# Hybrid encoder on one core: order of the mirrored Fourier rows, and smaller edits of the Fourier weights

## The chip, the cores and the metric

The kernel runs on one core of one Trainium2 chip. A core has five engines with a queue each: PE (TensorE, matmuls), DVE (VectorE), ACT (ScalarE), POOL (GpSimd) and SP (SyncE, which here only issues DMAs). The metric is the device time of one execution in microseconds (us); a run's result is compared by the median of several executions. The profile shows one execution. Its span runs from the first instruction to the last.

## The reference

Two layers over a sequence of 512 tokens of width 1024, in float32. Each layer is a half-step SwiGLU block, a mixer, and another half-step SwiGLU block; a final RMSNorm follows. The mixer is what the change touches:

```python
def fourier_mix(u):
    ug = u.astype(jnp.float32).reshape(B, T, F_GROUPS, F_GROUP_DIM)
    f = jnp.fft.fft2(ug, axes=(1, 3), norm="ortho").real
    return f.reshape(B, T, F_WIDTH).astype(u.dtype)

def mixer(h, w_in, gate_bias, rpb, w_na_out, w_f_out, w_o):
    z = h @ w_in                       # q, k, v, uf, ga, gf
    y_na = neighbourhood_attention(q, k, v, rpb) @ w_na_out
    y_f = fourier_mix(uf) @ w_f_out
    g_na = sigmoid(ga + gate_bias[0])
    g_f = sigmoid(gf + gate_bias[1])
    return (g_na * y_na + g_f * y_f) @ w_o
```

The neighbourhood attention has 8 heads of 64; the Fourier part has 4 groups of 128 channels; `ga` and `gf` are 1024 wide each.

## The kernel before

**Matmuls in three parts.** Every float32 operand of a large matmul is split into a high part (rounded to float32r, an ACT copy) and a low part (the rest, a DVE subtraction). A product is high times high, high times low and low times high. For weights, `Item.prep` makes the two parts `whi` (ACT, L207 or L202) and `wlo` (DVE, L210 or L203), each 128 x 1024, in three rotating buffers.

**Strassen products.** The large products are done by seven half-size products, numbered 1 to 7 (`strassen`, `product`). The weights come as granules of 128 x 1024 floats (512 KB), two per product. A granule serves 12 matmuls. Some products need sums of granules a, b, c, d: for product 7 the sum c + a, for product 5 the sum d + c, for product 6 that sum plus a, for product 3 also plus b. SP loads a granule from `wst` into a raw buffer (L155). `plus` then has POOL issue a DMA that adds a second granule to the buffer as it lands (L165); `then` (L212) does the same later, once the first use is over; other sums are made by DVE (L179).

**The stream of weights.** All items stand in one list. `Stream.prep` prepares items in order, and before each one fetches items up to `depth` (8) ahead. `next` hands out an item and prepares two items further. An item carries a stage number; it is not fetched before `enter` has raised the stage. In the mixer the raw buffers come from the shared pool of 23 buffers of 4 KB per partition (`slot`), which also holds activations, probabilities, Fourier results and the gate bias. `swap_pools(0)` closes the mixer's own pool and puts 9 raw buffers in its place; these serve the gates and the next block.

**Attention and Fourier part** (from L1695). PE, DVE and ACT run here in the order in which the program is written (`manual_schedule`). Eight blocks of attention (`Probs` 0 to 7: scores, `maxes`, `exps`, `inverse`, `scaled`, `transposed`, `kept`, and `att_pv` for two blocks at a time) are interleaved with the Fourier part:

- The transform along the tokens and channels uses symmetry. `four_high` and `four_ends` leave the even-odd halves `yf`, the end rows `e_` and the Nyquist column `nyq`.
- `part_f(0, ...)` multiplies the even half with the even weights (granules t1 + t2, added by POOL), and `part_f(1, ...)` the odd half with the odd weights (t1 - t2, loaded anew and subtracted by DVE). In `part_f(0, ...)` two more matmuls (L1653, L1654) bring in the end rows with the high and the low part of the ends' weights `fx`, which `ends_split` makes.
- `last_f` makes the Nyquist row in three partial products of 32 rows each; `f_last` copies them out of PSUM and has POOL add the three rows into row 3 of `fs[i, 0]` by DMAs of 2 KB.
- `f_both` makes, for each token, the sum into `gs` and the difference into `fs`. The rows of `gs` belong to mirrored tokens. `f_turn(i)` sends them to their places in `fs[i, .]` by eight DMAs on SP: four of 60 rows and four of 3 or 4 rows, 2 KB per row.

`i` is the half of the output columns (0 or 1).

**Gates.** `fill` multiplies attention's output with its first weights. Then `gate_block(0)` and `gate_block(1)` make both gates for a half of the columns each; block 0 takes its products in the order `FIRST`, block 1 in the order `ORDER`. After products 1 and 6 a `snap` copies the PSUM pair out by ACT (L619), and a later product adds to the same PSUM pair. `with_f` (product 7 and product 4) multiplies the gate into `fs` (DVE, L1539), so it needs the mirrored rows. `minus` and what follows it prepares the activations of products 5, 6, 7 and 4 (t1, t2, t3, t4). In this stretch DVE and ACT are ordered by the program only as far as its `manual_schedule` blocks reach; SP's order is not written out anywhere, the framework's scheduler sets it. Each engine runs its queue in order. After block 0, its two results are turned to channels by a DMA transpose on SP (`zt<-zs`, L376) and joined by ACT (L389).

In the program of before, `f_turn(0)`, `f_turn(1)` come at the end of the attention part, ahead of `fill`; the two bias loads `gb` (L1892) follow `fill`. They stand ahead of the loads of the gate's c granules.

Of the kernel before, what the change touches and what calls it, by code (L numbers as in the profile page):

```python
# [98 lines left out]
def encoder_kernel(  # L99
# [67 lines left out]
    class Item:  # L167
        def __init__(self, raw, add=None, neg=False, stage=0, parts=1, pieces=1, then=None, op=ALU.add):
            self.raw, self.add, self.neg, self.stage, self.parts, self.op = raw, add, neg, stage, parts, op
            self.pieces, self.then = pieces, then  # L170
# [6 lines left out]
        def summed(self):  # L177
            if self.add:
                V.tensor_tensor(self.raw.t, self.raw.t, self.add.t, self.op)  # L179
                self.add = None  # L180
# [14 lines left out]
        def prep(self, nxt):  # L195
# [8 lines left out]
            else:  # L204
                for c in range(0, n, n // self.parts):
                    cs = slice(c, c + n // self.parts)
                    S.activation(hi[:, cs], t[:, cs], AF.Copy)  # L207
                    if nxt:
                        nxt.summed()
                    self.last = V.tensor_tensor(lo[:, cs], t[:, cs], hi[:, cs].bitcast(F32), ALU.subtract)  # L210
# [6 lines left out]
    def stage_items():  # L217
# [5 lines left out]
        def strassen(s, name, idx, sizes, order, dma=False, behind=None):  # L223
# [4 lines left out]
            for q, q2 in (("a", None), ("b", None), ("c", "a"), ("d", "c")):  # L228
                r[q] = [Raw(key(q, g), n, q2 and key(q2, g)) for g, n in enumerate(sizes)]
# [5 lines left out]
            for m, g in at:  # L235
# [13 lines left out]
                else:  # L249
                    add(c)  # L250
# [19 lines left out]
        for l in range(L):  # L270
# [17 lines left out]
            for i in range(2):  # L288
                strassen(s, lambda q: "g" + q, i, two, ORDER if i else FIRST, True)
# [834 lines left out]
    def stage_mixer(l, norm, nxt):  # L1124
# [5 lines left out]
        ch = mp.tile([P, 164], F32, tag="ch", name=nm("ch"), bufs=1)  # L1130
# [221 lines left out]
        def four_high(ps, z):  # L1352
# [7 lines left out]
            def low_of():  # L1360
# [6 lines left out]
                V.tensor_copy(nyq[:, z, 0:1], ps[:, 256:257])  # L1367
# [4 lines left out]
        def four_ends(ps):  # L1372
# [7 lines left out]
            def low_of():  # L1380
                V.scalar_tensor_tensor(e_, g.bitcast(F32), ch[:, 162:163], t, ALU.mult, ALU.add)
                V.tensor_tensor(nyq[:, 2, 0:1], ps[:, 256:257], ch[:, 160:161], ALU.mult)
# [252 lines left out]
        def ends_split():  # L1635
            t = ends[0]
            h, l_ = hilo("fxh"), hilo("fxl")
            for i in range(2):
                S.activation(h[i], t[:, i], AF.Copy)
            for i in range(2):  # L1640
                V.tensor_tensor(l_[i], t[:, i], h[i].bitcast(F32), ALU.subtract)
            ends.extend([h, l_])

        def part_f(m, t, w, i=None):
# [7 lines left out]
            if m == 0:  # L1652
                PE.matmul(ps, e_[:, c], ends[1][i], start=False, stop=False)  # L1653
                PE.matmul(ps, e_[:, c], ends[2][i], start=False, stop=True)  # L1654
# [28 lines left out]
        def f_last(i, ps):  # L1683

            t = tmp(s="fl")
            V.tensor_copy(t[0:96], ps[0:96])
            to = fs[i, 0][3:4, 1, :]
            for z in range(3):
                row = t[32 * z : 32 * z + 1]
                if z == 0:  # L1690
                    G.dma_start(out=to, in_=row)
                else:
                    G.dma_start(out=to, in_=row, accum_op=ALU.add)

        with tc.manual_schedule(engines={mybir.EngineType.DVE, mybir.EngineType.Activation}):  # L1695
            with tc.manual_schedule(engines={mybir.EngineType.PE}):
# [71 lines left out]
                p[4].maxes(1)  # L1768
                q3 = q3()
# [24 lines left out]
                pf = [part_f(0, t, f_w[0], 0) for t in range(2)]  # L1794
                att_split(po[0])
# [7 lines left out]
                f_copy(0, 1, pf[1])  # L1803
                pt_[4] = kept(ts)
# [4 lines left out]
                att_split(po[1])  # L1809
                p[6].maxes(0)  # L1810
# [20 lines left out]
                for i in range(2):  # L1831
                    f_last(i, pl[i])
# [26 lines left out]
                f_turn(0)  # L1859
                f_turn(1)  # L1860
# [27 lines left out]
        bias = []  # L1888
        for which in range(2):
            b_ = slot(F32, "gb", (D,))  # L1890
            src = bass.AP(tensor=gbias.tensor, offset=gbias.offset + (2 * l + which) * D, ap=[[0, P], [1, D]])
            nc.sync.dma_start(out=b_, in_=src)  # L1892
            bias.append(b_)

# [9 lines left out]
        def fourth():  # L1904
            with behind_weights():
# [142 lines left out]
def _weights(g):  # L2048
    wst = np.zeros((len(GRAN), P, 1024), np.float32)
    for l in range(L):  # L2050
# [38 lines left out]
        for i in range(2):  # L2089
            four("g", i, ga, i * T, gf, i * T)  # L2090
            wf = g["f_w_out"][l][:, i * T : (i + 1) * T].reshape(4, P, T)
            for z in range(2):
                for e in range(2):
# [3 lines left out]
                    wst[GRAN_AT[s, "f", 4], 32 * (2 * z + e) : 32 * (2 * z + e) + 2, i * T : (i + 1) * T] = m[64]  # L2097
# [61 lines left out]
def _constants():  # L2159
# [12 lines left out]
    chan = np.zeros((P, 164), np.float32)  # L2172
    chan[:, 0:64], chan[:, 64:128] = np.cos(ca) / 256.0, np.sin(ca) / 256.0
    chan[:, 128:130] = (1.0 - 2.0 * (np.arange(P) % 2))[:, None] / 256.0
    chan[0::32, 160] = chan[0::32, 162] = 1.0
    chan[1::32, 161], chan[1::32, 162] = 1.0, -1.0
# [35 lines left out]
```

## Time and profile before

| | us |
|---|---|
| median of 3 runs | 1859.37 (1856.95 to 1862.17) |
| the profiled execution | 1860.03 |
| its span | 1858.3 |
| DVE busy | 1604.3 |
| ACT busy | 1306.1 |
| POOL busy | 187.7 |

The profile page gives the busy time of each engine and, in 40 slices of 46.5 us, its busy share in tenths. A timeline row gives start, duration, engine, line, operation, the tiles (output <- inputs, without buffer numbers), shapes and a count; in brackets stands the idle time of the engine just before and what ended it. In the chain of waits, each row is a piece of the chain that ended last: its start, its length and what it was. SPq rows are SP's issuing of DMAs; the transfer itself runs later. In a row of a stretch come the engines' busy times, then PE's granted clock (1.00 is full), the busy share of the DMA engines and what they moved in GB/s. Matmul durations overlap: at full clock one follows another every 0.227 us, though each is listed with 0.39.

### The profile page before, as it was taken

Reading aid. Unit: us, or ns where it says so; the run is one execution under the profiler, and the core shown is the slowest. Engines: PE = TensorE matmul, PEld = TensorE weight load, DVE = VectorE, ACT = ScalarE, POOL = GpSimd, SP = SyncE. Lnnn points to the kernel's source line nnn. Section 1 sums busy time; section 2 is a strip of 40 time slices with the busy share of each in tenths; the row PEclk is TensorE's granted clock in tenths of the full one; section 3 lists DMA queues with packets and bytes.
Section 4 is the critical chain, followed back from the end, with each engine's and each line's share of the span. In section 5 each row is a group of like instructions: output and inputs, shape, how many; then the busy total and the mean of one; then the engine's idle time right before and its main releaser. Section 6 shows DMA issues by size and latency. Waiting matters only on the chain.

```text
span 1858.3 us, 24537 instructions
## 1 busy us (share of the span) xinstructions
PE 1829.5 (98%) x8778; PEld 1514.2 (81%) x8778; DVE 1604.3 (86%) x1938; ACT 1306.1 (70%) x1775; POOL 187.7 (10%) x231
## 2 busy tenths in 40 slices
PE   9999999999899999999999999999998899999998
PEld 7888888887778888888888888888877788888886
DVE  7878899777889987889998888997788799888899
ACT  6777875677576777787667778666675677677865
POOL 0001010110111010001010100101011101110010
PEclk9999999999999999999999999999999999999999
DMA  9898799862987788869878986978539877888695
GB/s 304 223 242 213 187 280 285 205 199 85 283 217 183 167 229 241 215 198 279 249 190 214 226 224 202 282 251 226 160 124 273 214 181 177 219 232 215 200 286 157
DMA packets 206770, 405.87 MB, mean 218 GB/s; under 512 B 109116, under 2 KB 109276, under 8 KB 206648
## 3 DMA queue, kind: packets, MB, share of 16 engines
q1 hardware_dynamic: 176536, 302.61, 50.5%
q0 software_dynamic: 29680, 101.14, 29.9%
q8 instruction: 69, 1.13, 0.3%
q10 hardware_dynamic: 432, 0.55, 0.1%
q14 instruction: 53, 0.43, 0.1%
HBM read 372.76 MB, written 2.11 MB: 202 GB/s over the span
## 4 chain that ended last, share of the span: by engine, by line
PE 90%; DMA 4%; DVE 3%; ACT 2%; issue 1%; SPq 0%; ACTq 0%; DVEq 0%
PE A L534 10%; PE A L537 10%; PE A L535 10%; PE o L537 7%; PE o L534 7%; PE o L535 7%; PE B L534 5%; PE B L535 5%; PE B L537 5%; DMA raw<-in_wst_dram 2%; PE C L534 2%; PE C L535 2%; PE C L537 2%; PE ps L339 2%; PE ps L340 2%; PE ps L341 2%
## 5 line engine op out<-in xcount | busy, mean ns | idle before, releaser
L210 DVE TENSOR_TENSOR wlo<-raw,whi 128x1024 fp32r<-128x1024 f32 (+1 forms) x534 | 632.6, 1196 | 181.0 <-ACT whi L207 177.5
L207 ACT ACTIVATE whi<-raw 128x1024 fp32r<-128x1024 f32 (+1 forms) x534 | 546.7, 1033 | 292.4 <-PE A L535 60.4
L165 POOL DMA_DIRECT2D raw<-in_wst_dram x170 | 148.9, 895 | 1218.4 <-DMA raw<-in_wst_dram 636.3
L179 DVE TENSOR_TENSOR raw<-raw,raw 128x1024 f32<-128x1024 f32 (+1 forms) x152 | 181.6, 1197 | 2.0
L535 PE MATMUL A<-whi,xl 128*128 128x512 f32 x400 | 155.7, 389 | 0.0
L534 PE MATMUL A<-whi,xh 128*128 128x512 f32 x400 | 155.7, 389 | 0.0
L202 ACT ACTIVATE whi<-raw 128x1024 fp32r<-128x1024 f32 (+1 forms) x83 | 85.7, 1037 | 46.9 <-PE A L535 11.4
L389 ACT ACTIVATE at<-zt 128x1024 uint16<-128x1024 uint16 (+2 forms) x96 | 110.3, 1166 | 11.3 <-DMA zt<-zs 11.3
L537 PE MATMUL A<-wlo,xh 128*128 128x512 f32 x400 | 115.0, 389 | 0.0
L203 DVE SCALAR_TENSOR_TENSOR wlo<-raw,whi 128x1024 fp32r<-128x1024 f32 (+1 forms) x83 | 98.8, 1198 | 12.3 <-ACT whi L202 12.3
L537 PEld LDWEIGHTS A<-wlo,xh 128*128 128x128 f32 x400 | 75.1, 188 | 15.6
L534 PEld LDWEIGHTS A<-whi,xh 128*128 128x128 f32 x400 | 75.1, 188 | 15.4
L535 PEld LDWEIGHTS A<-whi,xl 128*128 128x128 f32 x400 | 75.1, 188 | 15.4
L534 PE MATMUL B<-whi,xh 128*128 128x512 f32 x208 | 81.2, 390 | 0.0
L535 PE MATMUL B<-whi,xl 128*128 128x512 f32 x208 | 81.0, 389 | 0.0
L535 PE MATMUL C<-whi,xl 128*128 128x512 f32 x208 | 81.0, 389 | 0.0
L534 PE MATMUL C<-whi,xh 128*128 128x512 f32 x208 | 80.9, 389 | 0.0
L370 ACT ACTIVATE zs<-th 128x1024 uint16<-128x1024 uint16 x80 | 79.4, 1040 | 0.4 <-DVE th L794 0.4
L787 ACT ACTIVATE th<-sn,rh 128x512 f32<-128x512 f32 x80 | 54.8, 715 | 31.2 <-DVE sn L624 30.3
L619 ACT ACTIVATE sn<-A 128x512 f32<-128x512 f32 x104 | 58.4, 584 | 22.9 <-PE A L537 22.9
L537 PE MATMUL C<-wlo,xh 128*128 128x512 f32 x208 | 59.8, 389 | 0.0
L537 PE MATMUL B<-wlo,xh 128*128 128x512 f32 x208 | 59.8, 389 | 0.0
(446 smaller groups left out, 4641.4 us busy)
## 6 DMA issues: line engine op xcount, KB each, us to landing
raw<-in_wst_dram SPq DMA_DIRECT2D x472, 512.0 KB, 6.0
raw<-in_wst_dram POOLq DMA_DIRECT2D x180, 512.0 KB, 8.1
bm<-in_bias_dram SPq DMA_DIRECT2D x16, 512.0 KB, 5.9
raw<-in_wst_dram SPq DMA_DIRECT2D x30, 256.0 KB, 5.9
vs<-v SPq DMA_DIRECT2D x24, 128.0 KB, 5.6
x<-in_xin_dram SPq DMA_DIRECT2D x4, 512.0 KB, 10.2
raw<-in_wst_dram POOLq DMA_DIRECT2D x8, 256.0 KB, 7.4
dft<-in_dft_dram POOLq DMA_DIRECT2D x8, 256.0 KB, 6.7
```

Source lines behind the costliest of these rows:

```text
L165: G.dma_start(out=self.t, in_=wst[GRAN_AT[self.plus]][:, 0 : self.n], accum_op=ALU.add)
L179: V.tensor_tensor(self.raw.t, self.raw.t, self.add.t, self.op)
L202: S.activation(hi, t, AF.Copy, scale=-1.0)
L203: self.last = V.scalar_tensor_tensor(lo, t, -1.0, hi.bitcast(F32), ALU.mult, ALU.subtract)
L207: S.activation(hi[:, cs], t[:, cs], AF.Copy)
L210: self.last = V.tensor_tensor(lo[:, cs], t[:, cs], hi[:, cs].bitcast(F32), ALU.subtract)
L370: S.activation(s[:, h], words[:, h], AF.Copy)
L389: S.activation(to[:, w], t[:, w], AF.Copy)
L534: PE.matmul(ps, lh, rh, start=start, stop=False, skip_group_check=again)
L535: PE.matmul(ps, ll, rh, start=False, stop=False, skip_group_check=again)
L537: PE.matmul(ps, lh, rl, start=False, stop=stop, skip_group_check=again)
L619: S.activation(t[:, b, :], ps[b], AF.Copy)
```

## The change

It has five parts.

1. **Mirrored rows and order.** `f_turn(0)` moves from the end of the attention part to the gates, behind the first three weights of `fill` and a new `ws.fetch(ws.prepped + 9)`. `f_turn(1)` moves into `fourth`, which runs after product 6 of gate block 0. The two bias loads move ahead of both.
2. **Odd Fourier weights in place.** t1 isn't loaded a second time. The raw buffer that holds t1 + t2 gets -2 x t2 added by one DVE instruction (`scalar_tensor_tensor`), after the even product and `last_f` have read it. `last_f(0)` comes earlier for this, right behind `part_f(0, ., 0)`; the second odd sum is called by hand after `p[7].maxes`.
3. **Ends' weights in one product.** The three products high x high, low x high and high x low of the end rows are laid in three rows of one matmul: the row of `fx` now stands three times, `ch` has one more column, and `ends_split` makes a tile with high, high and low parts in rows 0, 1 and 2 of each group of 32. One matmul in `part_f(0, ...)` goes, so four per layer.
4. **Nyquist row by DVE.** The Nyquist column stands in column 3 of `nyq`, so that the row comes out in row 3 of each 32. `f_last` copies 96 x 512 as before; two DVE additions over 32 x 512 write rows 0 to 31 of `fs[i, 0]`, and the later `f_turn` overwrites those that are not the Nyquist row.
5. **Order in the attention part.** The first two `minus` steps move from behind `p[7].scaled` to behind `p[4].maxes`; `ws.enter` comes before `p[7].maxes`; the second odd weight is prepared ahead of `p[7].scaled`. A new argument `on_chip` of `strassen` is passed as False and changes nothing.

```diff
@@ class Item
+                if self.twice:
+                    V.scalar_tensor_tensor(self.raw.t, self.add.t, -2.0, self.raw.t, ALU.mult, ALU.add)
+                else:
+                    V.tensor_tensor(self.raw.t, self.raw.t, self.add.t, ALU.add)
...
-                    if nxt:
+                    if nxt and not nxt.twice:
                         nxt.summed()
@@ stage_items
-            for t1, t2 in halves:
-                add(Raw(t1, plus=t2))
-            for t1, t2 in halves:
-                add(Raw(t1), Raw(t2), op=ALU.subtract)
+            even = [Raw(t1, plus=t2) for t1, t2 in halves]
+            for raw in even:
+                add(raw)
+            for raw, (_, t2) in zip(even, halves):
+                add(raw, Raw(t2), twice=True)
@@ four_high, four_ends
-                V.tensor_copy(nyq[:, z, 0:1], ps[:, 256:257])
+                V.tensor_copy(nyq[:, z, 3:4], ps[:, 256:257])
@@ ends_split
-            t = ends[0]
-            h, l_ = hilo("fxh"), hilo("fxl")
-            for i in range(2):
-                S.activation(h[i], t[:, i], AF.Copy)
-            for i in range(2):
-                V.tensor_tensor(l_[i], t[:, i], h[i].bitcast(F32), ALU.subtract)
-            ends.extend([h, l_])
+            t, h, z = ends[0], slot(F32R, "fxh", (2, T)), slot(F32, "fxz", (2, T))
+            S.activation(h, t, AF.Copy)
+            S.activation(z, t, AF.Copy, scale=ch[:, 163:164])
+
+            def low_of():
+                V.scalar_tensor_tensor(h, h.bitcast(F32), ch[:, 164:165], z, ALU.mult, ALU.add)
+
+            ends.append(h)
+            return low_of
@@ part_f
-                PE.matmul(ps, e_[:, c], ends[1][i], start=False, stop=False)
-                PE.matmul(ps, e_[:, c], ends[2][i], start=False, stop=True)
+                PE.matmul(ps, e_[:, c], ends[1][:, i], start=False, stop=True)
@@ f_last
-            t = tmp(s="fl")
+            t, to = tmp(s="fl"), fs[i, 0][0:32, 1, :]
             V.tensor_copy(t[0:96], ps[0:96])
-            to = fs[i, 0][3:4, 1, :]
-            for z in range(3):
-                row = t[32 * z : 32 * z + 1]
-                if z == 0:
-                    G.dma_start(out=to, in_=row)
-                else:
-                    G.dma_start(out=to, in_=row, accum_op=ALU.add)
+
+            def added():
+                V.tensor_tensor(to, t[0:32], t[32:64], ALU.add)
+                V.tensor_tensor(to, to, t[64:96], ALU.add)
+
+            return added
@@ attention part, in its order
                 p[4].maxes(1)
+                first = minus(B[0, 0], B[0, 1], "t1")
+                next(first)
+                next(first)
...
-                ends_split()
+                low = ends_split()
                 p[4].inverse(0)
                 p[4].inverse(1)
+                low()
...
                 pf = [part_f(0, t, f_w[0], 0) for t in range(2)]
+                pl = [last_f(0, raws[0])]
...
                 f_copy(0, 1, pf[1])
+                fl = f_last(0, pl[0])
...
                 att_split(po[1])
+                fl()
...
-                pl = [last_f(i, raws[i]) for i in range(2)]
+                pl.append(last_f(1, raws[1]))
+                ws.enter(ws.stage + 1)
                 p[7].maxes(0)
                 p[7].maxes(1)
+                ws.items[ws.prepped].summed()
...
-                for i in range(2):
-                    f_last(i, pl[i])
+                fl = f_last(1, pl[1])
...
                 p[7].inverse(1)
+                ws.prep(ws.pos + 2)
+                fl()
                 p[7].scaled(0)
                 p[7].scaled(1)
-                first = minus(B[0, 0], B[0, 1], "t1")
-                next(first)
-                next(first)
                 pt_[6] = kept(ts)
                 att_split(po[2])
-                ws.enter(ws.stage + 1)
...
                 f_both(1, 1, pf[1])
-                f_turn(0)
-                f_turn(1)
@@ gates
+        bias = []
+        for which in range(2):
+            b_ = slot(F32, "gb", (D,))
+            src = bass.AP(tensor=gbias.tensor, offset=gbias.offset + (2 * l + which) * D, ap=[[0, P], [1, D]])
+            nc.sync.dma_start(out=b_, in_=src)
+            bias.append(b_)
+
             w = [ws.next(0), ws.next(0)]
             ws.prep(ws.pos + 1)
+            ws.fetch(ws.prepped + 9)
+            f_turn(0)
             h1 = high(t12, "t1")
...
         def fourth():
+            f_turn(1)
             with behind_weights():
```

(The bias loads stood behind this block before.)

More of the change, by code (lines that the diff above doesn't have):

```diff
@@ L167, in encoder_kernel, with __init__ @@
     class Item:
[L168 to L169 removed]
+        def __init__(self, raw, add=None, neg=False, stage=0, parts=1, pieces=1, then=None, twice=False):
+            self.raw, self.add, self.neg, self.stage, self.parts, self.twice = raw, add, neg, stage, parts, twice
             self.pieces, self.then = pieces, then
@@ L221, in add, with strassen @@
             items.append(Item(*a, stage=st, **k))
-        def strassen(s, name, idx, sizes, order, dma=False, behind=None):
+        def strassen(s, name, idx, sizes, order, dma=False, behind=None, on_chip=False):
             def key(q, g):
@@ L228, in strassen @@
             for q, q2 in (("a", None), ("b", None), ("c", "a"), ("d", "c")):
-                r[q] = [Raw(key(q, g), n, q2 and key(q2, g)) for g, n in enumerate(sizes)]
+                plus = q2 and not (on_chip and q == "c")
+                r[q] = [Raw(key(q, g), n, key(q2, g) if plus else None) for g, n in enumerate(sizes)]
             d2 = [Raw(key("d", g), n) for g, n in enumerate(sizes)]
@@ L288, in stage_items @@
             for i in range(2):
-                strassen(s, lambda q: "g" + q, i, two, ORDER if i else FIRST, True)
+                strassen(s, lambda q: "g" + q, i, two, ORDER if i else FIRST, True, on_chip=False)
             for g in range(2):
```

25 lines of the change are left out of this document (10 added, 15 removed).

## The prediction

> **What bounds the kernel now.** First the page: the span, the engines' shares, the span in 40 slices.
>
> ```profile
> span 1858.3 us, 24537 instructions
> PE 1829.5 (98%) x8778; PEld 1514.2 (81%) x8778; DVE 1604.3 (86%) x1938; ACT 1306.1 (70%) x1775; POOL 187.7 (10%) x231
> ...
> PE   9999999999899999999999999999998899999998
> ```
>
> TensorE is busy 98% of the span. What a reordering can win is its idle time, and three slices show it: 10 (464 to 511 us), 30 and 31 (1394 to 1487). Both places lie where a mixer passes from attention to its gates. The waits of PE, then its timeline at those places, give the size:
>
> ```profile
> PE A L534 <- ACT sn L619: 19.1, 4, 6.1
> ```
> ```profile
> 496.73 0.79 PE L534 MATMUL A<-whi,t3h 128*128 128x512 f32 x1 [6.13 <-ACT sn L619]
> ...
> 502.04 0.39 PE L534 MATMUL A<-whi,t3h 128*128 128x512 f32 x1
> ...
> 541.17 0.50 PE L534 MATMUL A<-whi,t3h 128*128 128x512 f32 x1 [2.67 <-ACT sn L619]
> ...
> 1417.03 0.79 PE L534 MATMUL A<-whi,t3h 128*128 128x512 f32 x1 [5.59 <-ACT sn L619]
> ...
> 1420.35 0.39 PE L535 MATMUL A<-whi,t3l 128*128 128x512 f32 x1
> ...
> 1462.63 0.80 PE L534 MATMUL A<-whi,t3h 128*128 128x512 f32 x1 [4.69 <-ACT sn L619]
> ...
> 1468.40 0.39 PE L534 MATMUL A<-whi,t3h 128*128 128x512 f32 x1
> ```
>
> Four waits make 19.1 us, two in each layer, always before product 7: first in gate block 0, then in gate block 1. Each long wait is followed by slow matmuls. From 496.73 to 502.04 stand 12 matmuls in 5.31 us; 12 at the usual pitch of 0.227 (0.91 us for four) take 2.72, so 2.6 more are lost. In the same way 7 matmuls to 1420.35 lose 1.7 and 14 to 1468.40 lose 2.6; after the 2.67 gap none is lost. The first waits cost 8.7 and 7.3 us, the second 2.7 and 7.3: 26.0 in all.
>
> Who is late? The chain of waits through the first place, then SP's timeline:
>
> ```profile
> 469.45 6.68 DMA fs<-gs
> 476.15 7.03 DMA raw<-in_wst_dram
> 483.17 0.28 issue
> 483.46 11.57 DMA raw<-in_wst_dram
> 495.43 0.67 issue
> 496.10 0.59 ACT sn L619
> ```
> ```profile
> 453.64 2.79 SPq L1681 DMA_DIRECT2D fs<-gs  x3
> 456.53 3.86 SPq L155 DMA_DIRECT2D raw<-in_wst_dram  x6
> 460.43 13.61 SPq L1681 DMA_DIRECT2D fs<-gs  x13
> 474.14 0.83 SPq L1892 DMA_DIRECT2D gb<-in_gbias_dram  x2
> 475.02 35.04 SPq L155 DMA_DIRECT2D raw<-in_wst_dram  x13
> ```
>
> SP issues six weight loads (a, b, d of gate block 0), then spends 13.61 us on mirrored rows, then the two bias loads. Only at 475.02 come the two halves of c for product 7. They land 7 us later, POOL adds a to them (11.57 us for the second), ACT takes the high part, and the `snap` behind it in ACT's queue is what PE waits for. Layer 2 has the same chain.
>
> **The change part by part.** *Mirrored rows.* With `ws.fetch(ws.prepped + 9)` ahead of `f_turn(0)`, the halves of c stand behind the six loads and the bias loads: 460.4 + 0.8 + 2 x 0.64 (3.86 / 6) = 462.5 instead of about 476. Ten transfers of 0.5 MB from 456.5 at the 353 GB/s of the row below take 15 us, so c is there by 472, and with two additions of the page's median length
>
> ```profile
> raw<-in_wst_dram POOLq DMA_DIRECT2D x180, 512.0 KB, 8.1
> ```
> ```profile
> 480.00:490.00 10.00, 10.00 (x46) 8.28 (x45) 7.68 (x9) 3.23 (x5) 3.45 (x4) 1.00 1.03 353
> 490.00:500.00 10.00, 3.87 (x11) 2.55 (x10) 4.75 (x5) 4.85 (x6) 0.86 (x1) 0.76 1.06 251
> ```
>
> overlapping, the sum is ready near 480 to 484. ACT needs it by about 488, so that the snap follows product 6's end at 490.6 without a wait. Margin 4 to 8 us: both first waits go, 8.7 + 7.3 = 16.0 us. (The rows of this view: PE, PEld, DVE, ACT, POOL busy, granted clock, DMA share, GB/s.) Product 3 is late next: its weights get b by this POOL addition,
>
> ```profile
> 485.51 0.86 POOL L212 DMA_DIRECT2D raw<-in_wst_dram  x1 [1.19 <-DVE wlo L210]
> ```
>
> 8.1 us, so 493.6, against a need near 494 (product 7 takes 24 x 0.227 = 5.4 from 490.6, the high part 1.06 before that). I put 0.5 us per layer there, between nothing and 2.7 (the second wait of layer 1): +1.0.
>
> The moved rows still go somewhere. `f_turn(0)`, eight transfers, needs 6.7 us of SP (13.61 / 13 each, 0.8 counting only issue) behind c and must land before DVE's `with_f` of product 7,
>
> ```profile
> 509.62 1.22 DVE L1539 SCALAR_TENSOR_TENSOR fs<-sn,fs 128x1024 f32<-128x1024 f32 x1
> ```
>
> which is over 30 us of cover. `f_turn(1)` goes behind product 6 and holds SP for as long, with the weights of gate block 1 behind it. They are fetched eight ahead, 8 x 12 x 0.227 = 21.8 us; load 7.0 and addition 8.1 leave 6.7. That covers it, just; uncovered it would cost up to 6.7 us a layer. The bias loads now stand in front of c: 0.83 us of SP, counted above.
>
> *Attention.* Rows of the timelines of ACT, DVE and PE:
>
> ```profile
> 426.04 1.14 ACT L1639 ACTIVATE fxh<-fx 128x512 fp32r<-128x512 f32 x2
> 427.08 1.05 ACT L207 ACTIVATE whi<-raw 128x1024 fp32r<-128x1024 f32 x1
> ...
> 443.16 1.05 ACT L1468 ACTIVATE p<-ps 128x512 f32<-128x512 f32 x2
> ```
> ```profile
> 422.51 0.15 DVE L1382 TENSOR_TENSOR nyq<-ps,ch 128x1 f32<-128x1 f32 x1
> ...
> 426.69 1.29 DVE L1641 TENSOR_TENSOR fxl<-fx,fxh 128x512 fp32r<-128x512 f32 x2 [2.66 <-ACT fxh L1639]
> ...
> 436.62 2.35 DVE L179 TENSOR_TENSOR raw<-raw,raw 128x1024 f32<-128x1024 f32 x2
> ...
> 445.93 1.28 DVE L1686 COPY fl<-ps 96x512 f32<-96x512 f32 x2
> ...
> 449.01 1.22 DVE L1623 TENSOR_TENSOR t<-xl 128x1024 f32<-128x1024 f32 x1
> ```
> ```profile
> 432.47 0.39 PE L1654 MATMUL ps<-fxl,e 128*128 128x512 f32 x1
> ...
> 446.01 1.97 PE L1483 MATMUL ps<-p,vs 128*64 128x128 f32 x32
> ```
>
> The first two `minus` steps (2 x 1.14) move into DVE's idle 2.66 us before fxl: nothing there; without that cover, 2.4. The ends' weights now take two ACT passes over 1024 columns in place of two over 512: 2.0 for 1.1, so everything behind comes 1.0 later; DVE's one pass (1.2) equals its two. The odd weights in place: one pass for one (1.2, rows L179), and two loads of 0.5 MB a layer less, where the queues are idle anyway; but the second sum no longer covers the high part of the first (1.05 against 1.14 + waits), 0.1. Ahead of the maxima of block 6 then stand one fl copy (0.6) and two new adds over 32 x 512. No row has that shape: between 0.15 (one column) and 0.64 (half of row L1686); 96 partitions there take what 128 take in L1641, so I take 0.6 each, 1.2. Sum 1.0 + 0.1 + 0.6 + 1.2 = 2.9 us late into `maxes`, `exps` and `kept` of block 5, which ended at 444.2 for PE's `att_pv(2)` at 446.0: 1.8 of slack. PE comes 1.1 late per layer. The four dropped matmuls (L1654, 4 x 0.23 = 0.9) lie before this wait and only lengthen it. Bounds: -0.9 (nothing late) to 3.5 (the minus steps uncovered too): +2.2 for both layers, -1.8 to +7.0. POOL's three small transfers per half go at nothing (POOL 10% busy); the wider `ch`, `on_chip=False` and the earlier entry of the stage add no instruction on the path.
>
> *Second waits.* They end a chain through a transpose by DMA, whose code isn't touched:
>
> ```profile
> 529.80 9.51 DMA zt<-zs
> ```
> ```profile
> 1449.25 11.53 DMA zt<-zs
> ```
>
> I leave them: 0. Sum on the profiled execution's own 1860.03 (span 1858.3 and 1.7 around it): -16.0 + 1.0 + 2.2 = -12.8, 1847.2; the median of the runs lies 0.66 lower, so 1846.6. The rivals below are given on the median too.
>
> **The Trainium skill against this.** The trace shows DMA full, 1.03 and 1.06 in the rows above. The Trainium skill, "DMA: Bandwidth & Descriptors", section "Issuing engines are not separate DMA queues", holds that all transfers share the same 16 engines and that time saved in a sequencer is usually small beside the transfer. By that an earlier place in SP's queue would win little. It is the first rival, and SP's 13.61 us speak against it here. Its residual gap of about 3.2 us is priced without slow matmuls by the 2.67 row. "TensorE: Matmul & The Clock Gate", section "What's actually happening", of the Trainium skill puts the window of idleness before the clock halves at about 3.4 us; the traced gaps of 2.67 and 4.69 agree.
>
> **The rivals.**
> *DMA is the bound.* The weights then gain only what the rows took of the engines:
>
> ```profile
> fs<-gs SPq DMA_DIRECT2D x16, 120.0 KB, 4.4
> ```
>
> eight a layer, about 1.0 MB with the small ones, 2.9 us at 353 GB/s. The gaps become 3.2 and 2.7 and the slow matmuls go: -2.9 - 2.6 - 2.9 - 1.7 = -10.1, + 2.2: 1851.5. For it: DMA share above 1.0 from 480 on. Against: SP issued no weights for 14 us.
> *The second wait takes over.* PE arrives 7 us earlier, into a fuller DMA; layer 1's wait becomes layer 2's (7.3 for 2.7): + 4.6, 1851.2. Or calmer queues remove both: -10.0, 1836.6.
> *It doesn't do what it says.* SP's order isn't written out; already now three rows are issued before the six loads. If all rows stay in front, only attention's 2.2 remains: 1861.6.
> *Slower: the bias loads in front of c wait for a buffer.* They take two of the 23 shared buffers, earlier than now. SP is in order, so c waits too. It decides from c's issue later than 475. If the buffers come free only at about 480, with the third sum, each layer loses 5.1 + 1.1: 1871.8. For it: those buffers are crowded there. Against: at 474 the bias loads waited for nothing.
>
> **How the numbers follow.** Forecast 0.45; DMA bound 0.18; second wait grows 0.13, goes 0.12; not done 0.07; bias loads 0.05. The forecast alone reaches from 1841.6 (attention -1.8, product 3 at 0) to 1855.8 (+7.0 and 5.4); 1838 to 1858 takes in the two middle rivals with some spread and half of the calmer case; left out is about 0.18. A difference of 0.3%, 5.6 us, is about what a measurement of this kernel can tell: faster is below 1853.8. Faster: 0.45 + 0.12 + two thirds of 0.31 = 0.77; same: the rest and the not-done case, 0.17; slower 0.06.
>
> **What would show it.** SP's timeline: c's loads before the rows, near 462; PE's waits without the 6.13 and 5.59 rows; granted clock 1.00 from 490 to 510; `att_pv(2)` with a wait of 1 to 2 us; the second waits as before. Wrong if c comes early and product 7 still waits (DMA), if attention loses over 3 us, or if SP waits on the bias buffers.

## The result and the profile after

The changed kernel takes 1851.95 us, median of 13 runs (1847.3 to 1856.61), against 1861.51 for the kernel before, median of 13 runs taken beside them. The ratio is 0.9942, 95% interval 0.9927 to 0.9956: faster, by 0.6%. The forecast was 1846.6. The profiled executions stand 11.1 us apart, 1860.03 and 1848.91.

The page of the changed kernel: span, engines, PE in 40 slices.

```profile
span 1847.1 us, 24500 instructions
...
PE 1827.0 (99%) x8770; PEld 1508.3 (82%) x8770; DVE 1608.9 (87%) x1944; ACT 1307.6 (71%) x1775; POOL 179.6 (10%) x219
...
PE   9999999999999999999999999999999999999998
```

The three holes in PE's slices are gone. The waits of PE (in all, times, longest), then its timeline at the four old places:

```profile
PE A L539 <- ACT sn L624: 7.7, 4, 3.4
PE ps L345 <- DVE wlo L213: 1.2, 2, 0.8
```
```profile
497.78 0.50 PE L539 MATMUL A<-whi,t3h 128*128 128x512 f32 x1 [3.35 <-ACT sn L624]
...
537.92 0.50 PE L539 MATMUL A<-whi,t3h 128*128 128x512 f32 x1 [0.59 <-ACT sn L624]
...
1414.11 0.50 PE L539 MATMUL A<-whi,t3h 128*128 128x512 f32 x1 [2.81 <-ACT sn L624]
...
1452.95 0.50 PE L539 MATMUL A<-whi,t3h 128*128 128x512 f32 x1 [0.92 <-ACT sn L624]
```

None of the four waits is gone; all are shorter, 19.1 us have become 7.7. The first waits (3.35 and 2.81) were to vanish and did not. The second waits (0.59 and 0.92) were to stay and nearly vanished. A small new wait stands where the gates are merged (L345).

SP's timeline in layer 1:

```profile
456.14 2.33 SPq L155 DMA_DIRECT2D raw<-in_wst_dram  x5
458.51 0.92 SPq L1888 DMA_DIRECT2D gb<-in_gbias_dram  x2
459.47 1.21 SPq L155 DMA_DIRECT2D raw<-in_wst_dram  x2
461.00 15.04 SPq L1687 DMA_DIRECT2D fs<-gs  x8
```

The halves of c (the two loads at 459.47) now stand ahead of the rows, 15.6 us earlier than before. So the change does what it says. ACT's timeline and the chain of waits show what holds product 7 instead:

```profile
491.75 0.60 ACT L624 ACTIVATE sn<-A 128x512 f32<-128x512 f32 x1 [0.64 <-PE A L542]
496.19 1.06 ACT L210 ACTIVATE whi<-raw 128x1024 fp32r<-128x1024 f32 x1 [3.84 <-DMA raw<-in_wst_dram]
497.15 0.58 ACT L624 ACTIVATE sn<-A 128x512 f32<-128x512 f32 x1
```
```profile
488.57 7.51 DMA raw<-in_wst_dram
...
496.19 1.06 ACT whi L210
...
497.78 0.50 PE A L539
```

The two `sn` rows are the two halves of the copy (`snap`) after product 6. Between them stands a `whi` which product 7 does not need. It is the high part of product 3's first weights, and it waits for the addition of b that POOL issued at 488.57. ACT runs its queue in order. So the second copy, and with it all but the first 6 of product 7's 24 matmuls, waits for weights that are due only one product later.

### The profile page after: what moved, and what is told of

It reads as the page before. It is cut to its first block, busy times and chain, and to the rows that moved or that the text cites. A ratio compares the mean times of both kernels' runs of the same rounds, so it can differ in the third digit from the quotient of the medians.

```text
span 1847.1 us, 24500 instructions
## 1 busy us (share of the span) xinstructions
PE 1827.0 (99%) x8770; PEld 1508.3 (82%) x8770; DVE 1608.9 (87%) x1944; ACT 1307.6 (71%) x1775; POOL 179.6 (10%) x219
## 4 chain that ended last, share of the span: by engine, by line
PE 84%; DVE 5%; DMA 4%; issue 4%; ACT 3%; SPq 0%; POOL 0%; DVEq 0%; ACTq 0%; POOLq 0%
PE A L539 9%; PE A L540 9%; PE A L542 9%; PE o L542 7%; PE o L539 7%; PE o L540 7%; PE B L539 5%; PE B L540 5%; PE B L542 5%; DMA raw<-in_wst_dram 3%; PE C L540 2%; PE C L539 2%; PE C L542 2%; PE ps L344 2%; PE ps L345 2%
## 5 line engine op out<-in xcount | busy, mean ns | idle before, releaser
L182 DVE TENSOR_TENSOR raw<-raw,raw 128x1024 f32<-128x1024 f32 (+1 forms) x148 | 176.0, 1190 | 2.0
L542 PEld LDWEIGHTS A<-wlo,xh 128*128 128x128 f32 x400 | 75.1, 188 | 15.6
```

What stands on the lines that cost most here:

```text
L182: V.tensor_tensor(self.raw.t, self.raw.t, self.add.t, ALU.add)
L542: PE.matmul(ps, lh, rl, start=False, stop=stop, skip_group_check=again)
```

## The experiments

Each is set against the kernel before. The table compares the starts of the same matmuls in the trace of the kernel before and in that of the experiment: how much their distance grew over a stretch, in us, layer 1 / layer 2. "Attention" runs from the products ahead of the attention part to the gates' start, "first wait" from there to the middle of product 3 of gate block 0, "3 and 4" from there to product 6 of block 1, "second wait" to product 3 of block 1, "merge" to the first product behind the merge. One trace stands behind each row. Experiments 11 and 12 leave the first waits alone, and that column still reads +0.6 to +2.0 there: differences of up to 2 us between two rows say little.

| | ratio, 95% interval | attention | first wait | 3 and 4 | second wait | merge |
|---|---|---|---|---|---|---|
| changed kernel | 0.9942 (0.9927 to 0.9956) | +1.0 / +1.0 | -3.5 / -4.3 | 0 / 0 | -2.0 / -6.2 | +1.1 / +0.7 |
| 1 rows alone | 0.995 (0.9937 to 0.9963) | 0 / 0 | -2.9 / -0.6 | +0.1 / 0 | -2.6 / -5.5 | +2.1 / +0.4 |
| 2 the rest alone | 0.997 (0.9957 to 0.9983) | +1.0 / +1.0 | -0.8 / -0.7 | 0 / 0 | -2.3 / -7.0 | +1.5 / +1.9 |
| 3 copies first | 0.9916 (0.9901 to 0.9931) | +1.0 / +1.0 | -8.7 / -7.3 | +3.3 / +0.9 | -2.6 / -5.8 | +1.8 / +0.3 |
| 4 channels too | 0.9911 (0.9897 to 0.9925) | +1.0 / +1.0 | -8.7 / -7.3 | +3.7 / +0.9 | -2.9 / -7.4 | +2.1 / +1.3 |
| 5 as 4, old attention | 0.9955 (0.9938 to 0.9971) | 0 / 0 | -5.4 / -4.9 | +2.4 / +2.0 | -2.9 / -7.4 | +3.0 / +2.1 |
| 6 as 4, odd weights loaded | 0.9926 (0.9912 to 0.994) | +1.0 / +1.0 | -8.7 / -6.8 | +1.8 / +3.1 | -2.9 / -7.4 | +2.3 / +2.4 |
| 7 as 4, merge's weights first | 0.9909 (0.9893 to 0.9925) | +1.0 / +1.0 | -8.7 / -7.3 | +1.8 / +2.5 | -2.9 / -7.4 | +0.8 / 0 |
| 8 as 5 and 7, odd weights early | 0.992 (0.9906 to 0.9934) | -0.4 / -0.4 | -7.2 / -5.3 | +2.1 / +2.7 | -2.9 / -7.4 | +1.3 / +1.2 |
| 9 before, copies first | 0.9993 (0.9971 to 1.0016) | 0 / 0 | -0.9 / +0.3 | 0 / 0 | -1.4 / +0.3 | 0 / 0 |
| 10 changed, no early fetch | 0.9971 (0.9957 to 0.9986) | +1.0 / +1.0 | -0.6 / -1.4 | 0 / 0 | -1.4 / -7.0 | +0.6 / +1.5 |
| 11 before, channels behind | 0.9981 (0.9964 to 0.9998) | 0 / 0 | +2.0 / +0.6 | 0 / 0 | -1.9 / -0.3 | 0 / 0 |
| 12 before, transpose first | 0.9956 (0.994 to 0.9973) | 0 / 0 | +1.9 / +1.6 | 0 / 0 | -2.6 / -7.0 | 0 / +0.8 |

**1. The rows alone.** The kernel before with part 1 of the change.

```diff
-                f_turn(0)
-                f_turn(1)
...
             ws.prep(ws.pos + 1)
+            ws.fetch(ws.prepped + 9)
+            f_turn(0)
...
         def fourth():
+            f_turn(1)
```

> The kernel before with the first part of the change alone: the sixteen mirrored rows and the bias loads are issued behind the gates' first weights, with the earlier fetch; the attention's weights and the Nyquist row are made as before. If the moved rows do all of it (theory): both first waits of the gates shrink as in the changed kernel (8.7 to about 5 and 7.3 to about 2.8), the second waits shrink as well (2 and 6 us less), and the attention doesn't pay its +1.1 per layer: 1861.5 - 16.7 + 2, about 1847, ratio 0.992 (0.990 to 0.994). If the second waits shrink because of the other parts (the rival): only the first waits' 8.4 is left, 1853, ratio 0.9955.

1852.89 us, ratio 0.995. The number is the rival's, the split is neither's. The second waits shrank without the other parts, as the theory said. But the first waits gave less, because PE now stands earlier, in products 5 and 6, for low parts. PE's timeline:

```profile
483.10 1.21 PE L537 MATMUL B<-wlo,t1h 128*128 128x512 f32 x4 [0.71 <-DVE wlo L210]
...
491.10 1.19 PE L537 MATMUL A<-wlo,t2h 128*128 128x512 f32 x4 [1.14 <-DVE wlo L210]
```

**2. The rest alone.** The changed kernel with the rows, the fetch and the bias loads at their old places (the diff above, reversed).

> The changed kernel with the rows, the fetch and the bias loads back at their old places: only the attention's parts (odd weights in place, ends' weights in one product, Nyquist row on DVE) are left. Theory: first waits of 6.1 and 5.6 us before product 7 of the gates as in the kernel before, second waits as before, attention +1.1 per layer: ratio 1.001 (1.000 to 1.002). Rival (these parts free DMA or SP time that the second waits live on): second waits 6 to 8 us less in sum, ratio 0.997.

1858.17 us, ratio 0.997. The rival holds: the second waits lose 2.3 and 7.0 us here too. Attention costs 1.0 per layer, as foreseen. So the second waits shrink by either half of the change, though neither touches them.

**3. Copies first.** The changed kernel; ACT's instructions of product 7 are queued behind the second copy of product 6's sum. In ACT's order this exchanges one pair per layer, the high part and the copy.

```diff
                 elif m == 6:
...
+                    s2 = snap(pa)
+                    with tc.issue_after(snapped[0]):
                         with_n(arg(s1, 0, 0), 0)
...
                 elif m == 7:
+                    with tc.issue_after(snapped[0]):
                         product(pa, acts[7], K4, False, again=True)
```

> The changed kernel with one edge of order on ACT: the high parts of product 3's first weights stand behind both copies of product 6's sum, not between them. Theory 1 (the second copy stands behind a high part that waits for POOL's addition of b): the gaps of 3.35 and 2.81 us before product 7 go to under 0.5 us, the slow matmuls with them, and product 3 waits 1 us at most: 5 to 8 us less than the changed kernel's 1852, about 1845, ratio 0.991 (0.990 to 0.993). Theory 2 (the additions and loads are as late as the DMA queues allow, whatever waits for them): the gap moves to PE's first matmul of product 3, where PE waits 3 us for whi, and the time stays, ratio 0.994.

1847.7 us, ratio 0.9916. ACT's timeline:

```profile
492.40 0.60 ACT L626 ACTIVATE sn<-A 128x512 f32<-128x512 f32 x1 [0.64 <-PE A L542]
493.76 0.60 ACT L626 ACTIVATE sn<-A 128x512 f32<-128x512 f32 x1 [0.76 <-PE A L542]
497.56 1.06 ACT L210 ACTIVATE whi<-raw 128x1024 fp32r<-128x1024 f32 x1 [3.21 <-DMA raw<-in_wst_dram]
```

The high part waits for b as before, but the copy no longer stands behind it. The queues of SP, POOL and DVE hold the same order as in the changed kernel. Both first waits are gone in full, -8.7 and -7.3, just what the prediction had priced them at. So the cause that theory 1 names is shown. Its gain isn't: the median lies 4.2 us below the changed kernel's, not 5 to 8, and the two intervals still touch. Theory 2 holds for a part: products 3 and 4 give back 3.3 and 0.9 us.

**4. Channel copies too.** As 3, and `after[m]()`, which joins the channels, also under `issue_after(snapped[0])`.

> The experiment above, and the channel copies (mq from zt) of the second gate block as well behind the copy of the product's sum. By theory 1 the second waits left in the changed kernel (0.59 and 0.92 us) go too: about 1 us less than the experiment above, ratio 0.990 to 0.992; rival: the channels come late for the products that take them, and the wait moves into those (mq before a1), no gain or up to 2 us more.

1846.23 us, ratio 0.9911. The remaining second waits went (-2.9 and -7.4 in the table); against 3 the difference is inside the intervals. What is left at product 3 shows in PE's timeline, and the chain of waits behind it begins with the addition of b to product 3's second granule:

```profile
500.95 0.50 PE L539 MATMUL B<-whi,xh 128*128 128x512 f32 x1 [1.02 <-ACT whi L210]
```
```profile
489.38 10.36 DMA raw<-in_wst_dram
```

**5. The old attention with these orders.** Experiment 1 plus the orders of 3 and 4.

> The first experiment (rows, fetch and bias loads moved, attention as before) with the third and fourth one's order on ACT (high parts of product 3 behind both copies of product 6's sum, channel copies behind them too). If the attention's parts only cost (1.2 us per layer in the second experiment's trace): 1846.2 less 2.4, 1844, ratio 0.990. If they earn something, because the odd Fourier weights made in place need one load less for each half, so that the gates' weights come earlier: the low-part waits of products 5 and 6 of the first experiment (0.71, 0.80, 1.14 and 0.84, 1.13 us) stay, 1846.2 - 2.4 + 4.6, about 1848.5, ratio 0.9925.

1853.45 us, ratio 0.9955: even above the second case. No first gap is left, but the waits for low parts in products 5 and 6 stay. The attention's parts, which cost 1.0 per layer, earn more than that in the gates.

**6. Odd weights loaded anew.** As 4, with the loads of part 2 of the change undone; the earlier `last_f(0)` and the second sum called by hand stay.

```diff
-                    V.scalar_tensor_tensor(self.raw.t, self.add.t, -2.0, self.raw.t, ALU.mult, ALU.add)
+                    V.scalar_tensor_tensor(self.raw.t, self.add.t, -1.0, self.raw.t, ALU.mult, ALU.add)
...
-            for raw, (_, t2) in zip(even, halves):
-                add(raw, Raw(t2), twice=True)
+            for t1, t2 in halves:
+                add(Raw(t1), Raw(t2), twice=True)
```

> The fourth experiment (both orders on ACT) with one part of the attention's change undone: the odd Fourier weights are again made from two halves loaded afresh (two loads of 512 KB more per layer), not in place. If it is these loads that brought the gates' weights earlier, the low-part waits of products 5 and 6 come back (0.5 to 1.1 us each, as in the kernels with the attention as before) and the time is that of the fifth experiment plus what the other attention parts cost, 1851 to 1854, ratio 0.9945 to 0.996. If it is the Nyquist row's DMAs on POOL or the ends: no more than 1 us, 1847, ratio 0.9915.

1847.43 us, ratio 0.9926. My favoured case fails: the two loads saved per layer are worth 1.2 us between these medians, with overlapping intervals.

**7. The merge's weights first.** As 4; on DVE the work behind product 3 of block 1 stands behind the low part of the merge's first weights, for which PE waited in experiment 4:

```profile
552.06 0.50 PE L345 MATMUL ps<-wlo,o 128*128 128x512 f32 x1 [1.48 <-DVE wlo L213]
```
```diff
                     product(pa, acts[4], K4, False, again=True)
+                    if i == 1:
+                        with tc.issue_after(ws.items[ws.prepped - 2].last.ins):
+                            less(pb, s2)
+                            with_n(arg(s2, 0, 1), 1)
```

> The fourth experiment (both orders on ACT) with one more order, on DVE: in gate block 1 the differences and scalings after product 3 stand behind the low part of the merge's first weights, for which PE waited 1.48 and 0.99 us. Theory: these waits go, 2.5 us less than 1846.2, about 1844, ratio 0.990. Rival: what is put back (the gate's differences, the transposes of the merged gate) is late for the products that follow, and the time stays or grows, 0.991 or more.

1845.06 us, ratio 0.9909. These two waits are gone from the trace (merge +0.8 and 0 for +2.1 and +1.3), but against experiment 4 the time can't be told apart.

**8. Odd weights early, old attention.** As 5 and 7; the odd weights are prepared and the stage entered where the changed kernel does it, and `f_turn(0)` stands behind the last load on SP.

```diff
                 pl = [last_f(i, raws[i]) for i in range(2)]
+                ws.enter(ws.stage + 1)
...
                 p[7].inverse(1)
+                ws.prep(ws.pos + 2)
...
-            f_turn(0)
+            with tc.issue_after(loaded[0].ins):
+                f_turn(0)
```

> The fifth experiment (rows moved, attention as before, both orders on ACT) with the seventh one's order on DVE and two more orders: the odd Fourier weights are split two steps earlier and the gates' loads entered with them, as the changed kernel has it, and the rows of f_turn(0) stand behind all of these loads on SP, where three of them stood ahead (454.3 in the fifth experiment, loads from 457.2). If what the attention's part earned is this order alone (product 5's additions went out at 463 to 464 us with it, at 468 to 469 without): no low-part waits in products 5 and 6, and no attention cost: 1845.1 less 2.4, about 1842.5, ratio 0.9895. If it is the work saved (Nyquist row's DMAs, ends, one load less for each half): the waits stay, 1850 to 1853, ratio 0.994 to 0.9955.

1846.7 us, ratio 0.992: most of the way from 5 to 7, not the 1842.5 hoped for. POOL's first addition for product 5 in experiments 5, 8 and 4, one row of POOL's timeline each:

```profile
468.37 0.91 POOL L165 DMA_DIRECT2D raw<-in_wst_dram  x1 [14.34 <-PE ps L341]
```
```profile
465.03 0.91 POOL L167 DMA_DIRECT2D raw<-in_wst_dram  x1 [10.05 <-DMA raw<-in_wst_dram]
```
```profile
463.02 0.87 POOL L165 DMA_DIRECT2D raw<-in_wst_dram  x1 [73.41 <-DVE fs L1686]
```

SP's timeline of experiment 5 shows three rows of `f_turn(0)` in front of the gates' loads:

```profile
454.32 2.79 SPq L1685 DMA_DIRECT2D fs<-gs  x3
457.20 3.21 SPq L155 DMA_DIRECT2D raw<-in_wst_dram  x6
```

So most of what the attention's parts earn in the gates can be had by order alone, without their saved work. In 8 the gates' loads stand ahead of all rows, and the first addition goes out 3.3 us earlier than in 5. Experiment 8 made three edits together: the early odd weights and the early entry, which are of part 5 of the change, and the rows behind the loads. It has 7's order too. Which of them counts wasn't tried, nor why a wait of 1.1 us stays in product 6.

**9. The order of 3 on the kernel before.**

> The kernel before with the order on ACT alone: high parts of product 3's first weights behind both copies of product 6's sum. If the kernel before waits for the loads of c (the first copy stands behind product 7's high parts, which wait for them 5.20 and 3.02 us): the gaps of 6.13 and 5.59 us stay, ratio 0.999 to 1.000. If the order is the whole trouble: 8.7 and 7.3 us go, ratio 0.991.

1860.27 us, ratio 0.9993: no change. PE's timeline:

```profile
497.19 0.80 PE L534 MATMUL A<-whi,t3h 128*128 128x512 f32 x1 [5.87 <-ACT sn L621]
```

In the kernel before, the load of c itself was late. The order on ACT alone gains nothing there; in the changed kernel it does (experiment 3).

**10. The changed kernel without `ws.fetch(ws.prepped + 9)`.**

> The changed kernel without the line that fetches nine granules ahead; the rows stay where the change has them. SP then issues c's halves behind the eight rows of f_turn(0) (15 us of issues), at about 475 as before the change. If it is the fetch that brings c early: the first waits are back at 6 and 5.6 us, the time at 1857 to 1859, ratio 0.998. If the rows' place behind the first weights is enough: ratio 0.994 as for the changed kernel.

1856.36 us, ratio 0.9971. The first waits are back (6.25 and 4.16 us in its timeline, -0.6 and -1.4 in the table). The time is lower than expected because the second waits still shrink. c's high part was nearly in time, b's addition was not, and the second copy stands behind it as in the changed kernel. ACT's timeline:

```profile
490.31 1.06 ACT L210 ACTIVATE whi<-raw 128x1024 fp32r<-128x1024 f32 x1 [0.81 <-DMA raw<-in_wst_dram]
491.28 0.58 ACT L624 ACTIVATE sn<-A 128x512 f32<-128x512 f32 x1
498.42 1.06 ACT L210 ACTIVATE whi<-raw 128x1024 fp32r<-128x1024 f32 x1 [6.57 <-DMA raw<-in_wst_dram]
```

SP now issues c at 470.71. POOL issued b's addition no later than in the changed kernel (487.84 and 488.57), but it took 10.48 us where it took 7.51. That the loads pushed back to 470 lengthen it, by sharing the DMA engines with it, is likely; it wasn't tried by itself.

**11. Channel copies behind, on the kernel before.**

```diff
         def channels(j):
...
+            with tc.issue_after(snapped[0]):
                 joined_words(mq[0, j], turned[j])
```

> The kernel before with the channel copies alone (mq from zt) put behind the copies of the product's sum on ACT. If the second waits (2.7 and 7.3 us with their slow matmuls) come of a channel copy that stands ahead of the second copy and waits for the transpose: both go, 1861.8 - 10, ratio 0.9946 (0.994 to 0.996), the first waits as before. If the transposes are late for the products behind as well: PE waits elsewhere before the last product, ratio 0.998 or more.

1857.78 us, ratio 0.9981. The copy was moved, and in layer 2 its wait was not: the scheduler put another late instruction into the same slot. ACT's timeline:

```profile
1456.90 0.60 ACT L621 ACTIVATE sn<-A 128x512 f32<-128x512 f32 x1 [1.20 <-PE A L537]
1462.20 1.06 ACT L207 ACTIVATE whi<-raw 128x1024 fp32r<-128x1024 f32 x1 [4.70 <-DMA raw<-in_wst_dram]
1463.16 0.58 ACT L621 ACTIVATE sn<-A 128x512 f32<-128x512 f32 x1
```

This is the picture of the first waits again: a high part between the two copies.

**12. One exchange on SP, on the kernel before.** All kernels above whose second waits shrank in layer 2, the changed one among them, have two loads between the two transposes `zt` of a layer; the kernel before and experiments 9 and 11 have three. Here the third load is queued behind the second transpose (a counter in `Raw.load`, armed after the second `apart`). Nothing else changes in the order of any queue.

```diff
+                        turn[1] -= 1
+                        if turn[1] < 0:
+                            gate, turn[0] = turn[0], None
+                    with tc.issue_after(gate) if gate is not None else nullcontext():
                         nc.sync.dma_start(out=self.t[:, cs], in_=wst[GRAN_AT[self.key]][:, cs])
```

> The kernel before with one exchange in SP's queue per layer: the second transpose (zt) of the gates is issued ahead of the third load that stood between the two transposes, as every kernel of this study has it whose second waits were short. If that load is the cause: the second waits shrink from 2.7 and 7.3 us to about 1 each, the first waits stay, 1862 - 7.5, about 1854.5, ratio 0.996 (0.995 to 0.9975). If it is not (the DMA queues are as full either way): second waits as before, ratio 1.000.

1853.86 us, ratio 0.9956, as the theory said. SP's timeline and ACT's channel copy in the kernel before:

```profile
1443.34 1.87 SPq L376 DMA_TRANSPOSE zt<-zs  x1
1445.31 2.91 SPq L155 DMA_DIRECT2D raw<-in_wst_dram  x3
1449.25 4.18 SPq L376 DMA_TRANSPOSE zt<-zs  x1
```
```profile
1460.80 1.34 ACT L389 ACTIVATE mq<-zt 128x1024 uint16<-128x1024 uint16 x1 [4.49 <-DMA zt<-zs]
```

and in experiment 12:

```profile
1444.56 1.89 SPq L384 DMA_TRANSPOSE zt<-zs  x1
1446.55 1.58 SPq L163 DMA_DIRECT2D raw<-in_wst_dram  x2
1450.47 1.33 SPq L384 DMA_TRANSPOSE zt<-zs  x1
```
```profile
1457.43 1.36 ACT L397 ACTIVATE mq<-zt 128x1024 uint16<-128x1024 uint16 x1
```

From issue to landing the second transpose took 11.5 us before (1449.25 to 1460.80) and less than 7.0 now. It isn't issued earlier (1450.47 for 1449.25); what is gone is one load in front of it in the queue. Both second waits vanish from PE's waits. That accounts for the unforeseen gain: the change moved the transpose past one load by the way, because the scheduler orders SP anew for every program. The reverse, the third load put back in the changed kernel, wasn't tried.

**The best version** is experiment 7 with 1845.06 us, 0.9909 (0.9893 to 0.9925), faster than the changed kernel's 0.9942 (0.9927 to 0.9956), with intervals that just don't touch; 4 can't be told from it.

## Why the prediction came out near, with wrong terms

The sum was nearly right, -12.8 forecast against -11.1 between the profiles, but by luck: two errors of some 8 us cancel. The first waits with product 3 were to give -15.0 and gave -7.8; the second waits were to give nothing and gave -8.2. One of the prediction's own signs of being wrong came true: c came early and product 7 still waited.

- **c's loads before the rows: right.** 459.47, forecast 462.5.
- **Both first waits go, -16.0: right as a price, not yet in this kernel.** Experiment 3 shows -8.7 and -7.3. The changed kernel has -7.8 in both layers together.
- **Product 3 is late next, +0.5 per layer: the step that failed.** The landing of b's addition was well foreseen: 493.6 on the clock of before, 496.08 in the trace, whose gates start 2.4 us later. What I missed is who waits for it. I let only product 3 wait; but its high part stands in ACT's queue between the two copies on which product 7 waits, so the addition was due some 4 us earlier. The cost was 5.1 us in layer 1 (3.35, and 1.7 by 12 slow matmuls after it) and 2.81 in layer 2. Even with the order mended, products 3 and 4 cost 0.9 to 3.7 us per layer (experiments 3, 4 and 7), not 0.5. The same order on ACT stood in the trace of the kernel before, hidden behind c; ACT's timeline there:

```profile
496.10 0.58 ACT L619 ACTIVATE sn<-A 128x512 f32<-128x512 f32 x1
497.75 1.06 ACT L207 ACTIVATE whi<-raw 128x1024 fp32r<-128x1024 f32 x1 [1.07 <-DMA raw<-in_wst_dram]
498.71 0.58 ACT L619 ACTIVATE sn<-A 128x512 f32<-128x512 f32 x1
```

  In that trace the addition issued at 485.51 landed only just ahead of 497.75, some 12 us later, where the forecast took 8.1. The landing came out because it took 7.51 in the changed kernel.

- **Second waits unchanged, 0: wrong,** -2.0 and -6.2. I took "the code isn't touched" for "the time isn't touched". Experiment 12 gives the cause.
- **Attention +1.1 per layer: right in sum, not in place.** It is +1.0 and +1.0, and the two adds over 32 x 512 took 0.68 each where the estimate was 0.6. But all of it was to be one wait of 1 to 2 us at `att_pv(2)`. PE waits 0.16 us there, and 0.17 and 0.36 before the transposes of blocks 6 and 7, in both layers alike. Against the kernel before, PE falls back by 0.3, 0.4 and 0.9 us at these three places; the dropped matmuls give 0.9 back, and smaller shifts make up the rest. So the lateness reached blocks 6 and 7, which the prediction left out, and that the sum agrees is luck. PE's timeline after:

```profile
448.37 1.14 PE L1488 MATMUL ps<-p,vs 128*64 128x128 f32 x16 [0.16 <-ACT p L1473]
...
454.56 0.87 PE L1463 MATMUL ps<-ident,s 128*128 128x128 f32 x6 [0.36 <-ACT s L1455]
```

- **Nothing for the earlier entry of the stage: not borne out.** With the orders on ACT, the early odd weights, the entry and the rows behind the loads are worth 6.8 us together between medians (8 against 5, with 7's order on DVE in it); the entry alone wasn't tried.
- **f_turn(0) in 6.7 us of SP: mis-sized,** 15.04. By the prediction's own row, 13.61 for 13, eight take 8.4. c stood ahead of it; whether the 15 us cost something behind c wasn't tried.
- **Merge:** +1.1 and +0.7, not foreseen; PE arrives earlier there and waits for a low part of DVE's. The remainder, +1.1 us, lies in products that the change doesn't touch.

The rival "DMA is the bound" gave 1851.5 with gaps of 3.2 and 2.7, nearly the traced 3.35 and 2.81. It would have been easy to take that for its proof. But its price had no slow matmuls in it, and layer 1 has 1.7 us of them. And experiment 3 removes the gaps without a transfer less, so the full DMA set the length of the wait only together with ACT's order. The window rows after:

```profile
490.00:500.00 10.00, 6.65 (x26) 5.13 (x25) 7.06 (x8) 4.29 (x7) 1.71 (x2) 0.92 1.04 260
500.00:510.00 10.00, 10.00 (x42) 8.13 (x41) 8.16 (x9) 5.96 (x6) 1.69 (x2) 0.91 0.72 204
```

The granted clock is 0.92 and 0.91 where 1.00 was forecast: the 3.35 gap still slows the matmuls behind it.

The Trainium skill, "DMA: Bandwidth & Descriptors", section "Issuing engines are not separate DMA queues", counts the time that initiating a DMA takes on the sequencer as usually small beside the DMA itself. The trace agrees for each DMA by itself: c's two loads took 0.6 us of SP each, against a median of 5.7 from issue to landing for such loads, and the eight rows 1.9 each, against 16.9. The sentence doesn't speak of what stands behind a DMA in the same queue. That order was worth more here: one load moved past one transpose (12) gave 7.75 us between medians, c's loads ahead of the rows (10 against the changed kernel) 4.4.

## What to carry to other kernels

Where an engine's queue is in order, ask of each late instruction not only who needs its result but who stands behind it; one order on ACT removed 8.2 us of waiting here without a transfer less (experiment 3), 4.2 us of it net between medians. A scheduler that orders a whole program anew will also move transfers that an edit doesn't touch: compare the order of the DMA queue before and after, and price its differences. And a total that comes out right isn't evidence for its terms; here the rows alone and the rest alone each gained mostly through a wait that the prediction held fixed.

## What the runs showed of the hardware

A gap's length alone doesn't decide whether the clock falls. After 2.81 us in the changed kernel (above) no matmul was slow, and the granted clock is 1.00 in the stretch from 1410 to 1420. In experiment 2 a shorter gap, 2.44 us, is followed by a granted clock of 0.57, and 0.52 behind a further gap of 1.23. What else decides isn't shown. PE's timeline, then the rows of the two stretches:

```profile
1414.51 0.50 PE L539 MATMUL A<-whi,t3h 128*128 128x512 f32 x1 [2.44 <-ACT sn L624]
...
1418.27 0.80 PE L539 MATMUL A<-whi,t3h 128*128 128x512 f32 x1 [1.23 <-ACT sn L624]
```
```profile
1414.50:1418.30 3.80, 2.57 (x7) 1.51 (x7) 3.06 (x4) 1.63 (x3) 0.86 (x1) 0.57 1.05 274
1418.30:1422.00 3.70, 3.70 (x9) 2.93 (x10) 3.41 (x4) 1.92 (x2) 0.86 (x1) 0.52 1.09 295
```

The moved rows of 120 KB landed 16.9 us after their issue (median of 16), where they took 4.4 before the change. They now go out into full DMA engines, with c and its additions: the DMA share is 1.02 and 1.07 in the 10 us stretches from 460 and 470, where it was 0.36 and 0.90 from 450 and 460 before. The page's row after:

```profile
fs<-gs SPq DMA_DIRECT2D x16, 120.0 KB, 16.9
```
